# HGRN scores: copies of keys and queries for levels up to 32 tokens, and one run of matmuls for all levels of a pair of heads

## The chip, the cores and the metric

The kernel runs on one core of a Trainium2 chip. The metric is the device time in microseconds (us); before is the median of 3 runs. The engines each work through their own instructions in a fixed order and wait for each other by semaphores: PE is TensorE (matmuls; PEld is its loading of weights), DVE is VectorE, ACT is ScalarE, POOL is GpSimd, and SP issues the transfers (DMA).

## What is computed

A trunk of four residual layers over 256 tokens of width 1024: a token mixer, a layer norm, a SwiGLU block, a layer norm. The mixers are HGRN2, mLSTM, S5 and HGRN2 again, so the code of this change runs in the first and in the last layer. For HGRN2, a gated linear recurrence with 8 heads of 128, the reference forms in each chunk the scores that the kernel's `hgrn_scores` makes:

```python
b = jnp.cumsum(lfb, axis=2)
diff = b[:, :, :, None, :] - b[:, :, None, :, :]
decay = jnp.exp(jnp.where(mask[:, :, None], diff, -jnp.inf))
att = jnp.einsum('bhtd,bhsd,bhtsd->bhts', qb, kb, decay)
o = jnp.einsum('bhts,bhse->bhte', att, vb) + jnp.einsum('bhtd,bhde->bhte', qb * jnp.exp(b), s_prev)
```

The score of a query t and a key s is a dot product in which every one of the 128 channels is damped by the product of its forget gates between s and t. All is float32.

## The kernel before

The 256 tokens are two halves of 128. The heads are taken in four pairs; `q`, `k` and `f` of a pair are tiles of 128 channels x 512 (half, head of the pair, token). The products of gates are built by doubling. At level m (1, 2, 4, ... 64) the tokens fall into blocks of 2m; keys in the first m tokens of a block meet queries in the last m. Ahead of the level, keys hold the gates up to the end of their m tokens and queries those from the start of theirs, so that the level's scores are plain dot products. After it, DVE multiplies half the keys and half the queries by their neighbour's whole product (`mul(x, x, whose(...))`, in place, 128x256 each), and `e`, the products of whole blocks, is halved in length.

In `hgrn_scores` of before, a generator that gives up control after every level:

- The diagonal (key and query the same token) is 16 small matmuls into a bank (L649) and a masked multiply into `near` (L650).
- For m under 32, ACT copies the level's keys into `kk` (L659), TensorE does eight matmuls with 32 key columns and 32 query columns (L663) into a bank of their own, reading the queries with a stride straight from `q`, and DVE puts them under a mask into `near` (L666).
- For m = 32 and 64, eight small matmuls (L672) read `k` and `q` themselves; ACT copies the result into `att` (L679). At m = 32 DVE also copies the diagonal blocks from `near` into `att` (four 32x128 copies, L675).
- At m = 64 DVE multiplies the last half block; then two full 128x128 matmuls (L695) make the scores between the halves, which ACT copies out (`cross`, L697).

In the hardware's count a float32 matmul is two instructions, so eight matmuls show as x16.

`scores` runs the generators of two pairs of heads side by side: a step of one, a step of the other, then a piece of other TensorE work ("fill"): the queries of pairs 2 and 3 and the second half of the values v in the first call (pairs 0 and 1); `heads_out(0)` (att and cross times v, L543 and L545) and eight pieces of the output gate g in the second (pairs 2 and 3). Then come `turn` (gated heads transposed into `oh` and `ol`, L451 and L293), `heads_out(1)` and the output projection (L180 to L182 with `oh`, `ol`).

Weights come in transfers of 1 MB into tiles `w` (three buffers). ACT casts each half to `hi` (L149) and DVE takes the rest as `lo` (L150), eight buffers each; a wide product is three matmuls, L180 to L182. The order on each engine is made when the program is built, by a scheduler that may move instructions within their dependences; on the chip each engine keeps to it.

Of the kernel before, what the change touches and what calls it, by code (L numbers as in the profile page):

```python
# [9 lines left out]
F32 = mybir.dt.float32  # L10
F32R = mybir.dt.float32r
BF16 = mybir.dt.bfloat16
I32 = mybir.dt.int32
AF = mybir.ActivationFunctionType
# [3 lines left out]
P = 128  # L18
D = 1024
S = 256  # L20
KD = D // P
# [5 lines left out]
LN_EPS = 1e-5  # L27
HEAD_EPS = 1e-6
MASKED = (1, 2, 4, 8, 16)
BIG = 1e30  # L30
AHEAD = 1
ROWS = (0, 1, NBLK - 1)
# [2 lines left out]
class Trunk:  # L35
# [448 lines left out]
    def hgrn(self, j, gb, lb=None):  # L484

        nc, tc = self.nc, self.tc
        nw = self.const.tile([P, 1], F32, name=f"hnw{j}")
        with tc.tile_pool(name=self.uid("hg"), bufs=1, reuse_waits="tile") as hp, \
                tc.tile_pool(name=self.uid("hw"), bufs=2, reuse_waits="tile") as wp:
            msk = hp.tile([P, len(MASKED) + 1, 64], F32, name=self.uid("msk"))  # L490
            atts = [hp.tile([P, 512], F32, name=self.uid("att")) for _ in range(3)]
            for t in atts:
                nc.gpsimd.memset(t, 0.0)
            ot = self.transposed(hp)
            v = hp.tile([P, 2, D], F32, name=self.uid("v"))
            g = hp.tile([P, 2, D], F32, name=self.uid("g"))

# [61 lines left out]
            def turn(n, h):  # L559
                o, gate = on[n, h], g[:, h, n * 512 : (n + 1) * 512]  # L560
                nc.vector.tensor_tensor(o, o, gate, ALU.mult)
                self.head_turn(o, n, h, nw, ot, h == 1)

            mem, q, pre, on = {}, {}, {}, {}
# [8 lines left out]

            def scores(prs, fill):

                runs = [self.hgrn_scores(wp, q[pr], *pre[pr], msk, atts[pr % 3]) for pr in prs]
                for todo in fill:
                    for pr, run in zip(prs, runs):
                        mem[pr] = next(run)
                    for f in todo:  # L580
                        f()
# [11 lines left out]
            v1 = pieces(v, AF.Copy, 0, 1)  # L593
            g0, g1 = (pieces(g, AF.Silu, 12, n) for n in range(2))
            scores((0, 1), ([], [lambda: query(2)], [], [lambda: query(3)], v1[0:1], v1[1:2], v1[2:3], v1[3:]))
            late = []
            scores((2, 3), ([lambda: late.append(heads_out(0))], g0[0:1], g0[1:2] + [lambda: late.pop()()], g0[2:3], g0[3:], g1[0:1], g1[1:2], g1[2:3]))
            gb = gb()
            g1[3]()
            for h in range(2):  # L600
                turn(0, h)
            heads_out(1)()
# [19 lines left out]
                act(y, y, AF.Copy, scale=lb[:, 1, hd])  # L622
        return k, f

    def hgrn_scores(self, wp, q, k, f, msk, att):

        nc = self.nc
        mul = lambda o, x, y: nc.vector.tensor_tensor(o, x, y, ALU.mult)
        view = lambda t, o, *dims: bass.AP(t.tensor, t.offset + o, [list(t.ap[0])] + [list(d) for d in dims])
        i32 = lambda x: x.bitcast(I32)
        keys = lambda t, m: view(t, 0, (256 + m, 2), (2 * m, P // m), (1, m))
        queries = lambda t, m: view(t, m, (256 - m, 2), (2 * m, P // m), (1, m))
        whose = lambda e, m, s: view(e, s, (2 * P // m + 1 - 2 * s, 2), (2, P // m), (0, m))  # L640
        four = lambda x: x.rearrange("p (a t) -> p a t", a=4)
        heads = lambda x: x.rearrange("p (a t) -> p a t", a=2)
        rows = lambda c: slice(32 * c, 32 * c + 32)
        near = wp.tile([P, P], F32, tag="near", name=self.uid("near"))
        k4, q4, a4 = four(k), four(q), four(att)
        pd = self.bank("a")[:, 0:P]
        for i in range(4):
            for c in range(4):
                nc.tensor.matmul(pd[rows(c), rows(i)], k4[:, i, rows(c)], q4[:, i, rows(c)], start=True, stop=True)  # L649
        nc.vector.tensor_tensor(four(near), four(pd), msk[:, len(MASKED), None, 0:32].broadcast_to([P, 4, 32]), ALU.mult)  # L650
        mul(q, q, f)
        e, ends = f, wp.tile([P, 256], F32, tag="ends", name=self.uid("ends"))
        spare = 0
        for m in (1, 2, 4, 8, 16, 32, 64):
            n = P // (2 * m)
            pl = self.bank("a")
            if m < 32:
                kk = wp.tile([P, 2 * P], F32, tag="kk", name=self.uid("kk"))
                nc.scalar.copy(view(kk, 0, (m, 2), (2 * m, 2 * n), (1, m)), keys(k, m))  # L659
                pl = pl[:, 0:64]  # L660
                for i in range(2):
                    for c in range(4):
                        nc.tensor.matmul(pl[rows(c)].rearrange("p (h a t) -> p a h t", h=2, a=2)[:, i], kk[:, i * P + 32 * c : i * P + 32 * c + 32],  # L663
                                         view(q, i * P + 32 * c + m, (256 - m, 2), (2 * m, 16 // m), (1, m)), start=True, stop=True)
                three = lambda x: x.rearrange("p (h b m) -> p h b m", h=2, m=m)
                nc.vector.copy_predicated(view(near, m, (64 - m, 2), (2 * m, 32 // m), (1, m)), three(i32(msk[:, MASKED.index(m)])), three(pl))  # L666
            else:
                for i in range(2):
                    for c in range(4):
                        h = c * 32 // m % 2  # L670
                        t = 32 * c // (2 * m) * 2 * m + m * (1 - h)
                        nc.tensor.matmul(pl[rows(c), i * m : (i + 1) * m], k4[:, 2 * h + i, rows(c)], q4[:, 2 * h + i, t : t + m], start=True, stop=True)  # L672
                if m == 32:
                    for c in range(4):
                        nc.vector.tensor_copy(a4[rows(c), :, rows(c)], four(near[rows(c)]))  # L675
                for s in range(0, P, m):
                    h = s // m % 2
                    t = s + m * (1 - 2 * h)
                    nc.scalar.copy(a4[s : s + m, 2 * h : 2 * h + 2, t : t + m], heads(pl[s : s + m, 0 : 2 * m]))  # L679
            if m < 64:  # L680
                for x, y in ((keys(k, m), 1), (queries(q, m), 0)):
                    mul(x, x, whose(e, m, y))
                new = ends[:, 0 : 4 * n]
                if m > 1:
                    new, spare = f[:, spare : spare + 4 * n], spare + 4 * n
                mul(new, e[:, 0::2], e[:, 1::2])
                e = new
            else:
                for x, h in ((k4, 0), (q4, 2)):
                    x = x[:, h : h + 2, 0:m]  # L690
                    mul(x, x, e.rearrange("p (a s) -> p a s", s=2)[:, h : h + 2, 1:].broadcast_to([P, 2, m]))
            yield
        pc = self.bank("a")
        for i in range(2):
            nc.tensor.matmul(pc[:, i * P : (i + 1) * P], k4[:, i], q4[:, 2 + i], start=True, stop=True)  # L695
        cross = wp.tile([P, 2, P], F32, tag="cross", name=self.uid("cross"), bufs=3)
        nc.scalar.copy(cross, pc[:, 0:256].rearrange("p (a t) -> p a t", a=2))  # L697
        yield a4, cross
# [744 lines left out]
def consts():  # L1443
    s, c = np.arange(P)[:, None], np.arange(16)[None, :]
    lvl = []
    for m in MASKED:
        t = (c // m) * 2 * m + c % m
# [7 lines left out]
        "c_lvl": np.stack(lvl, 1).astype(np.float32),  # L1455
        "c_caus": np.where(s > t, np.float32(BIG), np.float32(0.0)),
    }
# [59 lines left out]
```

## Time and profile before

| | us |
|---|---|
| time, median of 3 runs | 1255.83 |
| lowest and highest | 1254.95, 1257.53 |
| span of the profiled execution, first to last instruction | 1251.8 |
| DVE multiplies of keys in the scores (48 of 128x256, the line of `mul`, L635) | 19.0 |
| ACT's key copies (40, L659) | 15.4 |
| DVE's masked copies (40, L666) | 10.2 |

Of the profiled execution the profile has only the span; the runs are timed around it. The scores of the first layer start with the diagonal at 52 us from the span's start (pairs 0 and 1) and at 82 us (pairs 2 and 3); the output projection follows at 118 us. In the last layer the diagonal of pairs 0 and 1 is at 971 us. In a row of the groups, the name before the arrow is written and those behind it are read, then come partitions x elements, the number of instructions, their busy time and mean in ns, and the idle time ahead of them with what ended it. A row of the timeline has the start, the duration (from the first start to the last end where several are merged), the engine, the line and the operation.

### The profile page before, as it was taken

Reading aid. Unit: us, or ns where it says so; the run is one execution under the profiler, and the core shown is the slowest. Engines: PE = TensorE matmul, PEld = TensorE weight load, DVE = VectorE, ACT = ScalarE, POOL = GpSimd, SP = SyncE. Lnnn points to the kernel's source line nnn. Section 1 sums busy time; section 2 is a strip of 40 time slices with the busy share of each in tenths; the row PEclk is TensorE's granted clock in tenths of the full one; section 3 lists DMA queues with packets and bytes.
Section 4 is the critical chain, followed back from the end, with each engine's and each line's share of the span. In section 5 each row is a group of like instructions: output and inputs, shape, how many; then the busy total and the mean of one; then the engine's idle time right before and its main releaser. Section 6 shows DMA issues by size and latency. Waiting matters only on the chain.

```text
span 1251.8 us, 21395 instructions
## 1 busy us (share of the span) xinstructions
PE 1234.0 (99%) x8464; PEld 1031.2 (82%) x8464; DVE 957.8 (77%) x1717; ACT 694.6 (55%) x1126; POOL 34.7 (3%) x60
## 2 busy tenths in 40 slices
PE   9999999999999999999998999999999999999997
PEld 7977788888788888888877788888889777888886
DVE  6887889796787799787599786666486887766664
ACT  6755575565467555555444355555359653555551
POOL 0000100000100100000000000000000000000000
PEclk9999999999999999999999999999999999999999
DMA  8733476666373278667556456555456433755530
GB/s 316 298 136 136 148 269 231 213 223 225 109 288 135 102 281 306 235 243 247 218 202 222 169 193 244 189 183 200 168 179 218 154 132 105 266 189 181 197 140 34
DMA packets 50245, 247.91 MB, mean 198 GB/s; under 512 B 6337, under 2 KB 15953, under 8 KB 23777
## 3 DMA queue, kind: packets, MB, share of 16 engines
q1 hardware_dynamic: 50016, 246.46, 54.7%
q8 instruction: 66, 1.08, 0.3%
q14 instruction: 35, 0.28, 0.1%
q0 software_dynamic: 128, 0.09, 0.0%
HBM read 233.94 MB, written 12.58 MB: 197 GB/s over the span
## 4 chain that ended last, share of the span: by engine, by line
PE 90%; DVE 5%; DMA 2%; ACT 2%; issue 0%; SPq 0%; DVEq 0%; ACTq 0%
PE g L210 18%; PE g L180 10%; PE g L182 10%; PE g L181 10%; PE g L213 9%; PE a L180 9%; PE a L181 8%; PE a L182 8%; DVE lo L150 1%; PE a L369 1%; PE t L271 1%; PE a L663 1%; DMA bc<-in_s_bc 1%; PE a L543 1%; DVE s5rot L1217 1%; DMA first<-in_first 1%
## 5 line engine op out<-in xcount | busy, mean ns | idle before, releaser
L150 DVE TENSOR_TENSOR lo<-w,hi 128x1024 fp32r<-128x1024 f32 x388 | 471.2, 1222 | 117.3 <-ACT hi L149 109.9
L149 ACT CAST hi<-w 128x1024 fp32r<-128x1024 f32 x388 | 405.5, 1051 | 187.5 <-PE a L181 100.6
L210 PE MATMUL g<-xx,hi 128*128 128x512 f32 x1024 | 356.7, 394 | 0.4 <-DVE sum L351 0.3
L213 PE MATMUL g<-xx,lo 128*128 128x256 f32 x1024 | 267.2, 281 | 0.0
L210 PEld LDWEIGHTS g<-xx,hi 128*128 128x128 f32 x1024 | 186.3, 188 | 36.1 <-DVE sum L351 1.1
L213 PEld LDWEIGHTS g<-xx,lo 128*128 128x128 f32 x1024 | 192.4, 188 | 11.0
L180 PE MATMUL g<-hi,xx 128*128 128x512 f32 (+1 forms) x416 | 167.5, 404 | 2.5 <-ACT xx L290 2.1
L182 PE MATMUL g<-lo,xx 128*128 128x512 f32 (+1 forms) x416 | 165.2, 399 | 0.1
L181 PE MATMUL g<-hi,xx 128*128 128x512 f32 (+1 forms) x416 | 164.6, 397 | 0.0
L180 PE MATMUL a<-hi,hh 128*128 128x512 f32 x328 | 129.5, 395 | 0.0
L350 ACT COPY sum<-g 128x256 f32<-128x256 f32 x128 | 47.7, 373 | 147.1 <-PE g L210 147.0
L182 PE MATMUL a<-lo,hh 128*128 128x512 f32 x328 | 129.1, 394 | 0.0
L181 PE MATMUL a<-hi,hl 128*128 128x512 f32 x328 | 128.9, 393 | 0.0
L351 DVE TENSOR_TENSOR sum<-g,sum 128x256 f32<-128x256 f32 x128 | 54.2, 423 | 63.5 <-ACT sum L350 62.9
L180 PEld LDWEIGHTS g<-hi,xx 128*128 128x128 f32 x416 | 78.3, 188 | 21.0 <-ACT xx L290 3.5
L182 PEld LDWEIGHTS g<-lo,xx 128*128 128x128 f32 x416 | 78.2, 188 | 18.2 <-DVE lo L150 1.4
L181 PEld LDWEIGHTS g<-hi,xx 128*128 128x128 f32 x416 | 78.4, 188 | 15.8
L182 PEld LDWEIGHTS a<-lo,hh 128*128 128x128 f32 x328 | 61.5, 188 | 14.5
L181 PEld LDWEIGHTS a<-hi,hl 128*128 128x128 f32 x328 | 61.5, 188 | 14.4 <-DVE hl L340 0.3
L180 PEld LDWEIGHTS a<-hi,hh 128*128 128x128 f32 x328 | 61.5, 188 | 12.6 <-ACT hh L339 0.2
L180 PE MATMUL g<-xx,hi 128*128 128x256 f32 x192 | 54.5, 284 | 0.0
L182 PE MATMUL g<-xx,hi 128*128 128x256 f32 x192 | 54.3, 283 | 0.0
(307 smaller groups left out, 1730.4 us busy)
## 6 DMA issues: line engine op xcount, KB each, us to landing
w<-in_w_gu SPq DMA_DIRECT2D x88, 1024.0 KB
w<-in_w_dn SPq DMA_DIRECT2D x44, 1024.0 KB
w<-in_w_hg SPq DMA_DIRECT2D x30, 1024.0 KB
w<-in_w_ml SPq DMA_DIRECT2D x12, 1024.0 KB
gb<-in_ln SPq DMA_DIRECT2D x8, 1024.0 KB
w<-in_w_ho SPq DMA_DIRECT2D x8, 1024.0 KB
w<-in_w_so SPq DMA_DIRECT2D x8, 1024.0 KB
w<-in_w_mo SPq DMA_DIRECT2D x4, 1024.0 KB
```

The costliest lines, as they stand in the source:

```text
L149: self.nc.scalar.copy(hi, x)
L150: i = self.nc.vector.tensor_tensor(lo, x, hi.bitcast(F32), ALU.subtract).ins
L180: mm(ps, lh, rh, start=start, stop=False)
L181: mm(ps, ll, rh, start=False, stop=False)
L182: mm(ps, lh, rl, start=False, stop=stop)
L210: whole = lambda: mm(ps, hi[:, c], self.xx[:, k].rearrange("p i t -> p (i t)"), start=k == 0, stop=k == KD - 1)
L213: mm(ps[:, S:], lo[:, c], self.xh[:, k], start=False, stop=False)
L271: nc.tensor.transpose(pt[:, (k % 4) * P : (k % 4 + 1) * P], z[:, k * P : (k + 1) * P], self.ident)
L350: nc.scalar.copy(t, ps[:, S:])
L351: nc.vector.tensor_tensor(t, ps[:, 0:S], t, ALU.add)
L369: nc.tensor.matmul(down[h][n], hidden(h, j, b)[x], dn[j][b][y][:, f], start=False, stop=(x, y, b) == steps[-1])
L543: nc.tensor.matmul(o, att[:, 2 * h + hd % 2, :], v[:, h, c], start=True, stop=h == 0)
```

## The change

Levels up to 32 (`NEAR`) no longer go to TensorE one by one. ACT copies the level's keys (as before) and now also its queries, into a tile of their own for each level: `big` (four levels, 2048 wide; named lev) and `kk` (two levels, 1024 wide). DVE multiplies `k` and `q` in place once they are copied. When the last multiply stands in the schedule, all matmuls of the pair follow: eight for m = 64, then eight for each of the six levels, 56 in all, into one bank at different columns. `self.order(...)` only tells the scheduler to place them behind that multiply. Then the masked copies for m under 32, the copies into `att` (those from `near` now on ACT instead of DVE) and, in place of DVE's two last multiplies, four on ACT (activation with a scale per channel). The generator still stops eight times. `big` shares its buffers with `oh` and `ol`, so these are made after the scores.

```diff
@@ def hgrn @@
-            ot = self.transposed(hp)
...
+            ot = tuple(hp.tile([P, KD, S], F32R, tag="o", name=self.uid(n), bufs=2) for n in ("oh", "ol"))
             for h in range(2):
                 turn(0, h)
@@ def hgrn_scores @@
+        big = hp.tile([P, 2048], F32, tag="o", name=self.uid("lev"), bufs=2)
+        kk = wp.tile([P, 1024], F32, tag="kk", name=self.uid("kk"))
+        saved = [t[:, i * 256 : (i + 1) * 256] for t, n in ((big, 8), (kk, 4)) for i in range(n)]
...
-        for m in (1, 2, 4, 8, 16, 32, 64):
+        for g, m in enumerate(NEAR):
             n = P // (2 * m)
...
+            kc, qc = saved[2 * g : 2 * g + 2]
+            nc.scalar.copy(view(kc, 0, (m, 2), (2 * m, 2 * n), (1, m)), keys(k, m))
+            nc.scalar.copy(view(qc, 0, (P, 2), (m, 2 * n), (1, m)), queries(q, m))
+            for x, y in ((keys(k, m), 1), (queries(q, m), 0)):
+                last = mul(x, x, whose(e, m, y)).ins
...
             yield
+        pl = self.bank("a")
+
+        def tiny(o, x, y):
+            self.order(nc.tensor.matmul(o, x, y, start=True, stop=True).ins, last)
+
+        for i in range(2):
+            for c in range(4):
+                h = c // 2
+                t = 64 * (1 - h)
+                tiny(pl[rows(c), 384 + i * 64 : 448 + i * 64], k4[:, 2 * h + i, rows(c)], q4[:, 2 * h + i, t : t + 64])
+        for g, m in enumerate(NEAR):
...
+                    tiny(o, x, y)
+        for g, m in enumerate(MASKED):
+            three = lambda x: x.rearrange("p (h b m) -> p h b m", h=2, m=m)
+            nc.vector.copy_predicated(view(near, m, (64 - m, 2), (2 * m, 32 // m), (1, m)), three(i32(msk[:, g])), three(pl[:, 64 * g : 64 * g + 64]))
+        for c in range(4):
+            nc.scalar.copy(a4[rows(c), :, rows(c)], four(near[rows(c)]))
+        for m, o in ((32, 320), (64, 384)):
...
+                nc.scalar.copy(a4[s : s + m, 2 * h : 2 * h + 2, t : t + m], heads(pl[s : s + m, o : o + 2 * m]))
+        for x, h in ((k4, 0), (q4, 2)):
+            for i in range(h, h + 2):
+                nc.scalar.activation(x[:, i, 0:64], x[:, i, 0:64], AF.Copy, scale=e[:, 2 * i + 1 : 2 * i + 2])
+        yield
```

The order that the scheduler makes of it, at three places of the first layer. TensorE in the first call of `scores`, before (`a` is a bank, the numbers tell tiles apart; q_559 is pair 0, q_620 pair 1; L180 to L182 are wide matmuls of the values):

```order
L663 MATMUL a_906<-q_559,kk_907 32x2x16 x8
L663 MATMUL a_921<-q_620,kk_922 32x2x16 x8
L180 MATMUL g_937<-hi_851,xx 128x512
L181 MATMUL g_937<-hi_851,xx 128x512
L182 MATMUL g_937<-lo_852,xx 128x512
L672 MATMUL a_960<-q_559,k_280 32x32 x8
L180 MATMUL g_936<-hi_940,xx 128x512
L672 MATMUL a_980<-q_620,k_349 32x32 x8
L181 MATMUL g_936<-hi_940,xx 128x512
```

And the same call now (L674 is the run; q_557 and lev_621 are pair 0, q_618 and lev_649 pair 1; the wide matmuls are L181 to L183 by the new file's lines):

```order
L183 MATMUL g_839<-lo_774,xx 128x512
L674 MATMUL a_884<-q_557,k_278 32x64 x8
L674 MATMUL a_884<-lev_621 32x2x16 x32
L674 MATMUL a_884<-kk_622 32x2x16 x8
L674 MATMUL a_884<-kk_622 32x32 x8
L674 MATMUL a_960<-q_618,k_347 32x64 x8
L674 MATMUL a_960<-lev_649 32x2x16 x32
L674 MATMUL a_960<-kk_650 32x2x16 x8
L674 MATMUL a_960<-kk_650 32x32 x8
L181 MATMUL g_838<-hi_842,xx 128x512
```

All level matmuls of the two pairs follow each other, with no wide matmul between; the queries of pairs 2 and 3 and half of the values have moved ahead of them.

DVE at the end of the second call, now (k_485 and q_826 are pair 3, near_1082 pair 2, on the heads' output, g the gate; before, each masked copy stood ahead of the next level's multiplies):

```order
L636 TENSOR_TENSOR k_485<-k_485,f_486 128x2x4x32
L636 TENSOR_TENSOR q_826<-q_826,f_486 128x2x4x32
L151 TENSOR_TENSOR lo_1489<-w_1486,hi_1488 128x1024
L151 TENSOR_TENSOR lo_1493<-w_1486,hi_1492 128x1024
L561 TENSOR_TENSOR on_1218<-on_1218,g_155 128x512
L561 TENSOR_TENSOR on_1220<-on_1220,g_155 128x512
L151 TENSOR_TENSOR lo_1581<-w_1578,hi_1580 128x1024
L695 COPY_PREDICATED near_1082<-msk_147,a_1312 128x2x32
L151 TENSOR_TENSOR lo_1585<-w_1578,hi_1584 128x1024
L695 COPY_PREDICATED near_1082<-msk_147,a_1312 128x2x16x2
L151 TENSOR_TENSOR lo_1603<-w_1600,hi_1602 128x1024
L695 COPY_PREDICATED near_1082<-msk_147,a_1312 128x2x8x4
```

The masked copies have moved behind the last multiplies and behind weights of the output projection. ACT at the same place, before (L679 copies into att, g is the gate, oh the turned heads):

```order
L679 COPY att_150<-a_1376 32x2x32 x4
L679 COPY att_148<-a_1396 32x2x32 x4
L149 CAST hi_1602<-w_1600 128x1024
L679 COPY att_150<-a_1440 64x2x64 x2
L679 COPY att_148<-a_1453 64x2x64 x2
L149 CAST hi_1606<-w_1600 128x1024
L697 COPY cross_1481<-a_1478 128x256
L697 COPY cross_1486<-a_1483 128x256
L149 CAST hi_1640<-w_1638 128x1024
L93 ACTIVATE g_157<-g_1416 128x512
L149 CAST hi_1644<-w_1638 128x1024
L93 ACTIVATE g_157<-g_1417 128x512
```

And now (L705 is the scaling that DVE did, L697 and L702 the copies into att, L711 cross):

```order
L705 ACTIVATE k_485<-k_485,f_486 128x64 x2
L705 ACTIVATE q_826<-q_826,f_486 128x64 x2
L697 COPY att_150<-near_1082 32x4x32 x4
L702 COPY att_150<-a_1312 32x2x32 x4
L702 COPY att_150<-a_1312 64x2x64 x2
L697 COPY att_148<-near_1110 32x4x32 x4
L702 COPY att_148<-a_1388 32x2x32 x4
L702 COPY att_148<-a_1388 64x2x64 x2
L711 COPY cross_1479<-a_1476 128x256
L711 COPY cross_1484<-a_1481 128x256
L150 CAST hi_1606<-w_1600 128x1024
L150 CAST hi_1640<-w_1638 128x1024
```

All copies into att stand in one row behind the scalings, and two casts of the output projection's weights have moved behind them.

More of the change, by code (lines that the diff above doesn't have):

```diff
@@ L29 @@
 MASKED = (1, 2, 4, 8, 16)
+NEAR = MASKED + (32,)
 BIG = 1e30
@@ L574, in scores @@
             def scores(prs, fill):
-                runs = [self.hgrn_scores(wp, q[pr], *pre[pr], msk, atts[pr % 3]) for pr in prs]
+                runs = [self.hgrn_scores(hp, wp, q[pr], *pre[pr], msk, atts[pr % 3]) for pr in prs]
                 for todo in fill:
@@ L623, in hgrn_gates, with hgrn_scores @@
         return k, f
-    def hgrn_scores(self, wp, q, k, f, msk, att):
+    def hgrn_scores(self, hp, wp, q, k, f, msk, att):
         nc = self.nc
@@ L652, in hgrn_scores @@
         e, ends = f, wp.tile([P, 256], F32, tag="ends", name=self.uid("ends"))
-        spare = 0
-        for m in (1, 2, 4, 8, 16, 32, 64):
+        spare, last = 0, None
+        for g, m in enumerate(NEAR):
             n = P // (2 * m)
[L656 to L691, printed above, removed]
-            yield
@@ new lines, in hgrn_scores @@
+            kc, qc = saved[2 * g : 2 * g + 2]
[3 more added lines that the diff above has]
+                last = mul(x, x, whose(e, m, y)).ins
+            new = ends[:, 0 : 4 * n]
+            if m > 1:
+                new, spare = f[:, spare : spare + 4 * n], spare + 4 * n
+            mul(new, e[:, 0::2], e[:, 1::2])
@@ new lines, in hgrn_scores @@
+            e = new
+            yield
+        pl = self.bank("a")
[7 more added lines that the diff above has]
+        for g, m in enumerate(NEAR):
+            kc, qc = saved[2 * g : 2 * g + 2]
+            for i in range(2):
+                for c in range(4):
+                    x = kc[:, i * P + 32 * c : i * P + 32 * c + 32]
+                    o = pl[rows(c), 64 * g : 64 * g + 64]
+                    if m < 32:
+                        o = o.rearrange("p (h a t) -> p a h t", h=2, a=2)[:, i]
+                        y = view(qc, (4 * i + c) * 16, (P, 2), (1, 16))
+                    else:
+                        o, y = o[:, rows(i)], qc[:, c % 2 * P + (2 * i + c // 2) * 32 :][:, 0:32]
+                    tiny(o, x, y)
@@ new lines, in hgrn_scores @@
+        for g, m in enumerate(MASKED):
+            three = lambda x: x.rearrange("p (h b m) -> p h b m", h=2, m=m)
+            nc.vector.copy_predicated(view(near, m, (64 - m, 2), (2 * m, 32 // m), (1, m)), three(i32(msk[:, g])), three(pl[:, 64 * g : 64 * g + 64]))
+        for c in range(4):
+            nc.scalar.copy(a4[rows(c), :, rows(c)], four(near[rows(c)]))
+        for m, o in ((32, 320), (64, 384)):
+            for s in range(0, P, m):
+                h = s // m % 2
+                t = s + m * (1 - 2 * h)
+                nc.scalar.copy(a4[s : s + m, 2 * h : 2 * h + 2, t : t + m], heads(pl[s : s + m, o : o + 2 * m]))
```

## Prediction

> **What bounds the kernel now.** The page comes first: how long, which engine is busy, and what the chain of waits ends on.
>
> ```profile
> span 1251.8 us, 21395 instructions
> PE 1234.0 (99%) x8464; PEld 1031.2 (82%) x8464; DVE 957.8 (77%) x1717; ACT 694.6 (55%) x1126; POOL 34.7 (3%) x60
> PE 90%; DVE 5%; DMA 2%; ACT 2%; issue 0%; SPq 0%; DVEq 0%; ACTq 0%
> ```
>
> TensorE sets the end: 99% busy, 90% of the chain. So an edit pays only if it shortens TensorE's own sequence, and costs only if TensorE comes to wait. The groups show little to gain: the level matmuls of the scores are busy for 11.1 us in 640 instructions (two per matmul).
>
> ```profile
> L663 PE MATMUL a<-q,kk 128*32 128x32 f32 x640 | 11.1, 200 | 0.0
> ```
>
> But a busy mean of pipelined matmuls hides what lies between two starts. The timeline of TensorE shows it, around a group of 16 such instructions, one of 32, and one of 32 with 64 columns (start, duration):
>
> ```profile
> 94.75 0.40 PE L181 MATMUL g<-hi,xx 128*128 128x512 f32 x1
> 95.07 0.46 PE L663 MATMUL a<-q,kk 128*32 128x32 f32 x32
> 95.46 0.50 PE L182 MATMUL g<-lo,xx 128*128 128x512 f32 x1
> 95.80 0.39 PE L180 MATMUL g<-hi,xx 128*128 128x512 f32 x1
> 96.03 0.39 PE L181 MATMUL g<-hi,xx 128*128 128x512 f32 x1
> ...
> 98.57 0.40 PE L181 MATMUL g<-hi,xx 128*128 128x512 f32 x1
> 98.90 0.33 PE L663 MATMUL a<-q,kk 128*32 128x32 f32 x16
> 99.16 0.50 PE L182 MATMUL g<-lo,xx 128*128 128x512 f32 x1
> 99.50 0.39 PE L180 MATMUL g<-hi,xx 128*128 128x512 f32 x1
> ...
> 104.05 0.40 PE L182 MATMUL g<-lo,xx 128*128 128x512 f32 x1
> 104.38 0.65 PE L672 MATMUL a<-q,k 128*32 128x64 f32 x32
> 104.96 0.50 PE L180 MATMUL g<-hi,xx 128*128 128x512 f32 x1
> 105.30 0.39 PE L181 MATMUL g<-hi,xx 128*128 128x512 f32 x1
> ```
>
> Two wide matmuls start 0.23 us apart (95.80 to 96.03). With a group of 16 between, three starts span 98.57 to 99.50: 0.93 less two wide intervals is 0.47 us. With 32, 94.75 to 95.80 gives 0.59. So 16 more cost 0.12 (7.5 ns each), and **entering and leaving the narrow shape costs 0.33 to 0.35 us** whatever the group's size; I take 0.33. By the same fixed part, the 64-column group (1.25 - 0.46 = 0.79) costs 14 ns an instruction.
>
> **The change part by part.** *Fewer switches.* In the order of before, the two calls of the scores of a layer enter the narrow shape 12 and 11 times; in the new order 3 and 3 times (the diagonal blocks of two pairs of heads in one or two groups, one run for both pairs; in the second call one or a few matmuls of the run stand alone). The instructions are as many as before: 32 + 96 + 16 a pair. The full-size cross matmuls are wide and pay no switch in either. So 17 x 0.33 = 5.6 us a layer, **11.2 us in both**, if nothing waits.
>
> *What must be ready at the run.* Instead of one level's copy, the run needs all six rounds of ACT copies and DVE multiplies of both pairs. Marks of before, then DVE and ACT at work there (start to start is what a row occupies):
>
> ```profile
> 52.18 0.46 PE L649 MATMUL a<-q,k 128*32 128x32 f32 x32
> ...
> 58.55 0.28 PE L181 MATMUL a<-xx,lo 128*128 128x256 f32 x1
> ...
> 64.00 0.28 PE L182 MATMUL a<-xx,hi 128*128 128x256 f32 x1
> ...
> 82.31 0.46 PE L649 MATMUL a<-q,k 128*32 128x32 f32 x32
> ...
> 117.81 0.48 PE L180 MATMUL g<-hi,oh 128*128 128x512 f32 x1
> ...
> 123.50 0.63 PE L451 MATMUL t<-ident,on 128*128 128x128 f32 x4
> ```
>
> ```profile
> 52.71 0.29 DVE L650 TENSOR_TENSOR near<-a,msk 128x128 f32<-128x128 f32 x1 [0.99 <-PE a L649]
> 52.92 0.68 DVE L635 TENSOR_TENSOR q<-q,f 128x512 f32<-128x512 f32 x1
> 53.52 0.42 DVE L635 TENSOR_TENSOR k<-k,f 128x256 f32<-128x256 f32 x1
> 53.85 1.22 DVE L150 TENSOR_TENSOR lo<-w,hi 128x1024 fp32r<-128x1024 f32 x1
> ```
>
> ```profile
> 64.82 0.70 ACT L659 COPY kk<-k 128x256 f32<-128x256 f32 x2
> 65.42 1.05 ACT L149 CAST hi<-w 128x1024 fp32r<-128x1024 f32 x1
> 66.37 0.40 ACT L659 COPY kk<-k 128x256 f32<-128x256 f32 x1
> ```
>
> DVE, both pairs: twice 0.21 + 0.60, 24 multiplies of 0.33, one lo of 1.2, and some 1.5 for the ten smaller products of the ends: 12.2 us, with 0.5 of waits for ACT 12.7, so to 65.4. ACT's 22 copies at 0.30 to 0.33 and two or three casts at 0.95 take 9 to 10 us beside it. TensorE now does queries 2 and 3 first: 96 matmuls at 0.12 ((64.00 - 58.55) / 46), 24 wide ones at 0.23 and the diagonal blocks, 18.3 us, so it is at the run at 70.4, with 5 us in hand. In the last layer one piece of v stands before the diagonal blocks, which takes 3.0 us of this cover: 2 us in hand. First runs: nothing.
>
> *Behind the first run.* ACT holds a cast until TensorE has freed its buffer (70.4). Then come 8 scalings 128x64, two key copies, 8 copies 32x128, 8 of 32x64, 4 of 64x128, a cast and two cross copies, and heads_out of the next call wants att and cross. The 32x64 and 64x128 copies are in the trace; the 32x128 copy stood on DVE (0.22), and the scaling was DVE's 128x128 multiply, half as often.
>
> ```profile
> L675 DVE COPY att<-near 32x128 f32<-32x128 f32 x32 | 6.9, 216 | 0.3
> ...
> 74.52 1.72 ACT L679 COPY att<-a 32x64 f32<-32x64 f32 x8
> ...
> 77.34 1.09 ACT L679 COPY att<-a 64x128 f32<-64x128 f32 x4
> L93 ACT ACTIVATE k<-k,lb 128x256 f32<-128x256 f32 x8 | 3.9, 494 | 0.0
> ```
>
> A scaling lies between 0.22 (the 32x64 copy) and 0.49 (four times the elements with a scale); I take 0.25, near the copy, 0.27 for the 32x128 copy. Sum 0.95 + 2.0 + 0.7 + 2.2 + 1.7 + 1.1 + 0.95 + 0.7 = 10.3, to 80.7. TensorE arrives at 80.0 and needs the first cross 0.9 later: no wait, but no slack; at 0.49 a scaling it waits 1.7.
>
> *Second run.* DVE's new chain stands behind a lo that waits for the cast after those copies, so it begins near 81 and, with two reductions and two scalings of heads_out among its rows, reaches the last multiply of pair 2 after 12.5 to 13.5 us, 94. TensorE arrives after heads_out (2.7) and 54 wide matmuls (12.6) at 95.4: no wait in layer 0. In the last layer the cast comes later against TensorE's place (v's evictions ahead of it) and a lo stands among the last multiplies: there 2 us of wait.
>
> *The tail.* After the second run DVE does five lo and two gate products (8 us) before the ten masked copies end; ACT then has both pairs' copies (5.0), two crosses, three casts, two gates and the first oh: 10.2 us from 103.4, so oh comes at 113.6. TensorE, 5.2 us ahead of before by then, wants it at 112.8 and ol 0.6 after: 1.2 to 1.5 us of wait, against none before (117.81 follows heads_out at once). From there oh, the squares, their reductions and GpSimd's power set the next turn:
>
> ```profile
> 121.46 1.29 DVE L555 TENSOR_TENSOR on<-a,rs 128x512 f32<-128x512 f32 x2 [2.05 <-POOL rs L223]
> ```
>
> that turn (123.50 before) I put at 120.0, so 3.5 us are kept in layer 0; in the last layer 5.6 - 2 - 1.3 = 2.3.
>
> *A long narrow run* can outrun TensorE's instruction supply, as in the S5 layer:
>
> ```profile
> 655.06 1.09 PE L1201 MATMUL g<-s5u,bm 128*32 128x64 f32 x63
> 656.79 1.23 PE L1201 MATMUL g<-s5u,bm 128*32 128x64 f32 x65 [0.64 <-issue]
> ```
>
> Nothing at best (a run of 128 elsewhere has no gap), 0.64 in each of four runs at worst, 2.6 us; where TensorE waits for the tail anyway it is hidden. I take 0.2 net. DVE loses 32 copies and 16 multiplies, covered by TensorE either way. The output tiles oh and ol move into the level buffers and are written after both runs: nothing.
>
> **Sum.** 11.2 less 2.1 (layer 0), 3.3 (last layer) and 0.2 leaves 5.6 us: span 1251.8 to 1246.2. The runs shown (1254.95 to 1257.53, median 1255.83) lie 4.0 over the span, so **1250.2 us**.
>
> **Rivals.** *The tail takes it all.* If what now stands behind a run on ACT costs more (0.49 for each of 8 scalings, 0.15 more for each of 16 small copies: 4.3 us), oh comes as late as 117.81 and both layers end where they did: 1255.8. For it speaks that the small copies of two pairs lay among the levels' casts and gates and now all wait for the run; against it, that oh has 4 us to lose. The Trainium skill, "TensorEngine Tiling (Array Packing)", section PSUM Bottleneck, says that packing speeds up TensorE but not the emptying of PSUM, which may become the bottleneck, and advises both ScalarE and VectorE for it, where this change puts more on ScalarE; by that rule the time is this rival's. No row of before shows the emptying as TensorE's bound there, which is why it gets the smaller chance.
>
> *Slower: the chain paces.* Each multiply must wait for ACT's copy of the same round, and each copy for the round before. I have two pairs overlap fully (1.6 us a round). If a weight cast in ACT's queue and the hand-overs make a round 2.4, six rounds grow by 4.8: with 5, 1.4, 2 and -2 us in hand, TensorE waits 0, 3.4, 2.8 and 6.8, 13 us against 11.2 gained, with the tail's 2.6: about 1260. It turns slower from a round of 2.2 on. Against it: a copy and a multiply of one tensor take 0.40 + 0.42, so even one pair alone turns in under 1.6.
>
> *It keeps nearly all.* If ACT's scalings and copies are as short as 0.2 and the casts fall in gaps, the waits vanish: 1244.6 to 1247.
>
> *Same work, same switches.* If the 0.33 belonged to waits for the copies and not to the shape, merging would save little: 1254 to 1256. Against it: 16 and 32 instructions give the same fixed part.
>
> **Chances.** Forecast (1247 to 1253.3) 0.50; nearly all kept 0.17; eaten by the tail or no switch cost 0.23; slower 0.10. A measurement tells 0.2%, 2.5 us, from no change: faster 0.67, same 0.23, slower 0.10. The range leaves out the very best and the slow case: 1245 to 1257.
>
> **What would show it.** Right: 12 entries into the narrow shape instead of 46; the second call beginning near 80.0 instead of 82.31 and out_proj near 114 with a wait of about 1 us for oh; 2 us before the last layer's second run. Wrong: waits of over 2 us at a run for q or k; a narrow instruction at over 8 ns in a run; gaps of issue within it; heads_out waiting for att or cross; or oh at 117 or later.

## The result, and the profile after

| | us |
|---|---|
| before, median of 4 runs beside it | 1255.66 (1254.95 to 1257.53) |
| after, median of 4 runs | 1264.87 (1262.25 to 1265.97) |
| ratio | 1.0073, 95% interval 1.0060 to 1.0086 |
| predicted | 1250.2, range 1245 to 1257 |

The change makes the kernel slower by 9.2 us, where 5.6 us of gain were forecast. The profiled execution has a span of 1262.1 us against 1251.8. Its page, the lines that answer to the first three of before:

```profile
span 1262.1 us, 21401 instructions
PE 1228.8 (97%) x8464; PEld 1033.9 (82%) x8464; DVE 947.3 (75%) x1669; ACT 728.3 (58%) x1246; POOL 39.1 (3%) x60
PE 81%; DVE 8%; ACT 4%; DMA 3%; issue 2%; POOL 1%; SPq 0%; DVEq 0%; ACTq 0%; POOLq 0%
```

TensorE has as many instructions as before and is busy for 5 us less, but its share of the chain fell from 90% to 81%: it now waits. "Issue", time in which it waited for nothing that the profile names, rose from 0% to 2%. The waits of TensorE's queue, longest in total first (what waited, for what, total us, times, longest):

```profile
PE a L674 <- issue: 8.7, 2, 4.6
PE g L181 <- ACT g L94: 4.4, 2, 3.2
...
PE a L653 <- ACT att L702: 1.2, 1, 1.2
...
PE a L709 <- issue: 0.6, 1, 0.6
PE t L452 <- DVE on L561: 0.3, 1, 0.3
```

L674 is the line of the run. Two of its four runs, both in the first layer, stop in the middle. The timeline of TensorE around the first of them:

```profile
76.71 0.39 PE L674 MATMUL a<-kk 128*32 128x32 f32 x21 [4.16 <-issue]
77.02 0.79 PE L181 MATMUL g<-hi,xx 128*128 128x512 f32 x1
77.61 0.63 PE L182 MATMUL g<-hi,xx 128*128 128x512 f32 x1
78.04 0.63 PE L183 MATMUL g<-lo,xx 128*128 128x512 f32 x1
78.47 0.63 PE L181 MATMUL g<-hi,xx 128*128 128x512 f32 x1
...
80.75 0.39 PE L181 MATMUL g<-hi,xx 128*128 128x512 f32 x1
```

A run of both pairs leaves 448 records, 224 of matmuls and 224 of weight loads; 21 of the matmul records were still to come when TensorE stood for 4.16 us. The layer's second run stops further from its end:

```profile
111.33 0.38 PE L674 MATMUL a<-lev 128*32 128x32 f32 x11 [4.56 <-issue]
```

Behind the first gap the wide matmuls start 0.43 us apart (77.61 to 78.04), not 0.23. The same stretch by windows (the length, the busy us and instructions of PE, PEld, DVE, ACT and POOL, then the granted TensorE clock, the share of DMA time and GB/s):

```profile
70.00:72.00 2.00, 2.00 (x165) 1.79 (x164) 1.94 (x3) 1.86 (x5) 0.00 (x0) 1.00 0.93 336
72.00:74.00 2.00, 0.55 (x57) 0.43 (x47) 1.64 (x6) 1.90 (x8) 0.00 (x0) 1.00 1.00 406
74.00:76.00 2.00, 0.00 (x0) 0.00 (x0) 0.00 (x0) 1.83 (x8) 0.00 (x0) 1.00 1.01 389
76.00:78.00 2.00, 1.29 (x23) 1.10 (x24) 0.79 (x3) 0.55 (x3) 0.00 (x0) 0.75 0.42 176
78.00:80.00 2.00, 2.00 (x6) 1.57 (x5) 0.50 (x3) 1.30 (x5) 0.00 (x0) 0.50 0.05 12
80.00:82.00 2.00, 2.00 (x11) 1.69 (x11) 0.00 (x0) 1.81 (x7) 0.00 (x0) 0.90 0.00 0
```

Two things are to be seen. The DMA engines are full (1.00) for as long as TensorE stands, with weights. And after the gap the clock is granted at 0.50 until about 80, which costs another 1.6 us (eight starts in 3.50 us, 77.02 to 80.52, where 1.9 would do). So the second call of the scores begins late:

```profile
52.08 0.46 PE L653 MATMUL a<-q,k 128*32 128x32 f32 x32
...
85.23 0.76 PE L653 MATMUL a<-q,k 128*32 128x32 f32 x64
...
126.06 0.48 PE L181 MATMUL g<-hi,oh 128*128 128x512 f32 x1
...
979.26 0.95 PE L653 MATMUL a<-q,k 128*32 128x32 f32 x64
...
1043.64 0.47 PE L181 MATMUL g<-hi,oh 128*128 128x512 f32 x1
```

From the first diagonal to the output projection the first layer takes 73.98 us (65.63 before), the last 64.38 (62.57 before, 971.17 to 1033.74): 8.35 and 1.81, together 10.2, where the span grew by 10.3. The switches were saved: 6 and 5 entries into the narrow shape instead of 23 and 23, 11.6 us at 0.33. Lost were 8.7 in the two gaps, about 4 in half clock (behind both gaps and behind the wait of 3.2), 5.6 in waits for ScalarE (4.4 for a gate activation, 1.2 for att) and 0.9 more (0.6 and 0.3). That makes 7.6 of 10.2. The 2.6 us that are left may lie in the price of a switch: at 0.28 us, as experiment 8 shows it, 9.8 are saved and not 11.6, and 0.8 are left.

### The profile page after: what moved, and what is told of

The parts are those of the page before. It is cut to its first block, busy times and chain, and to the rows that moved or that the text cites. A ratio compares the mean times of both kernels' runs of the same rounds, so it can differ in the third digit from the quotient of the medians.

```text
span 1262.1 us, 21401 instructions
## 1 busy us (share of the span) xinstructions
PE 1228.8 (97%) x8464; PEld 1033.9 (82%) x8464; DVE 947.3 (75%) x1669; ACT 728.3 (58%) x1246; POOL 39.1 (3%) x60
## 4 chain that ended last, share of the span: by engine, by line
PE 81%; DVE 8%; ACT 4%; DMA 3%; issue 2%; POOL 1%; SPq 0%; DVEq 0%; ACTq 0%; POOLq 0%
PE g L211 18%; PE g L214 9%; PE g L181 8%; PE g L183 8%; PE g L182 8%; PE a L182 8%; PE a L181 8%; PE a L183 8%; DVE lo L151 2%; ACT hi L150 1%; PE a L370 1%; PE t L272 1%; DMA bc<-in_s_bc 1%; PE a L674 1%; DVE s5rot L1231 1%
## 5 line engine op out<-in xcount | busy, mean ns | idle before, releaser
L181 PE MATMUL g<-hi,xx 128*128 128x512 f32 (+1 forms) x416 | 168.9, 407 | 6.9 <-ACT g L94 4.4
L182 PE MATMUL g<-hi,xx 128*128 128x512 f32 (+1 forms) x416 | 165.1, 398 | 0.0
L183 PE MATMUL g<-lo,xx 128*128 128x512 f32 (+1 forms) x416 | 164.9, 398 | 0.1
L181 PE MATMUL a<-hi,hh 128*128 128x512 f32 x328 | 129.5, 395 | 0.0
L183 PE MATMUL a<-lo,hh 128*128 128x512 f32 x328 | 129.2, 394 | 0.0
L182 PE MATMUL a<-hi,hl 128*128 128x512 f32 x328 | 128.8, 393 | 0.0
L181 PEld LDWEIGHTS g<-hi,xx 128*128 128x128 f32 x416 | 79.3, 191 | 26.7 <-ACT g L94 5.3
L183 PEld LDWEIGHTS g<-lo,xx 128*128 128x128 f32 x416 | 79.2, 191 | 18.9 <-DVE lo L151 1.4
L182 PEld LDWEIGHTS g<-hi,xx 128*128 128x128 f32 x416 | 79.4, 191 | 16.1
L183 PEld LDWEIGHTS a<-lo,hh 128*128 128x128 f32 x328 | 61.5, 188 | 14.5
L182 PEld LDWEIGHTS a<-hi,hl 128*128 128x128 f32 x328 | 61.5, 188 | 14.3 <-DVE hl L341 0.2
L181 PEld LDWEIGHTS a<-hi,hh 128*128 128x128 f32 x328 | 61.5, 188 | 12.5 <-ACT hh L340 0.2
L181 PE MATMUL g<-xx,hi 128*128 128x256 f32 x192 | 54.5, 284 | 0.1
L183 PE MATMUL g<-xx,hi 128*128 128x256 f32 x192 | 54.3, 283 | 0.0
```

The lines of the kernel that those rows point to most:

```text
L181: mm(ps, lh, rh, start=start, stop=False)
L182: mm(ps, ll, rh, start=False, stop=False)
L183: mm(ps, lh, rl, start=False, stop=stop)
```

## The experiments

**The theories.** F (fetch): TensorE's instructions themselves come by DMA, in blocks, and a long run of short instructions uses up what is loaded while the next block waits behind weights. Its page row is

```profile
q8 instruction: 66, 1.08, 0.3%
```

66 packets of 16 KB for TensorE's 2 x 8464 = 16,928 records: 256 instructions a packet. The run of two pairs is 448 instructions in 2.4 us; wide ones would last 256 x 0.117 = 30 us. The windows from the span's start to either gap count what TensorE had issued (matmuls and weight loads):

```profile
0.00:72.60 72.60, 71.16 (x732) 63.26 (x732) 56.47 (x92) 57.44 (x94) 1.79 (x9) 1.00 0.77 284
0.00:106.80 106.80, 100.00 (x1112) 86.48 (x1113) 79.20 (x151) 82.00 (x159) 6.10 (x11) 0.98 0.60 222
```

1464 and 2225: 761 apart, three blocks of 256 less a few records that a trace can miss. The gaps stand at the same place of a block. Up to the first gap the instruction queue had moved four packets, up to the second seven: three more here too. Rivals: L (length: any long run of narrow matmuls stalls), W (a wait that the profile doesn't name, at those matmuls), and C (the extra copies on ScalarE are the real loss, and the gaps stand where TensorE would wait anyway).

The table has all runs; the second and third columns are the time from the first diagonal to the output projection in the first and last layer, read from the timelines as above.

| | first layer | last layer | median | ratio to before, 95% |
|---|---|---|---|---|
| before | 65.63 | 62.57 | 1254.6 to 1255.7 | |
| after | 73.98 | 64.38 | 1264.87 | 1.0073 (1.0060 to 1.0086) |
| 1 shifted | 69.67 | 67.83 | 1262.97 | 1.0061 (1.0046 to 1.0076) |
| 2 halves | 67.20 | 64.45 | 1260.60 | 1.0038 (1.0025 to 1.0051) |
| 3 loads held | 70.19 | 64.41 | 1262.14 | 1.0058 (1.0042 to 1.0075) |
| 4 no run, all copies | 66.42 | 70.02 | 1264.90 | 1.0079 (1.0064 to 1.0094) |
| 5 levels by twos | 62.92 | 60.13 | 1250.27 | 0.9963 (0.9949 to 0.9978) |
| 6 halves, less on ScalarE | 65.99 | 60.33 | 1253.65 | 0.9984 (0.9975 to 0.9994) |
| 7 run, less on ScalarE | 73.81 | 61.07 | 1262.52 | 1.0062 (1.0046 to 1.0078) |
| 8 levels by twos and three | 61.78 | 58.81 | 1247.77 | 0.9941 (0.9924 to 0.9958) |

The intervals of 1, 3, 4 and 7 overlap that of after: there the verdict is read from the trace, not from the time.

**1. The run shifted against the blocks.**

```diff
     for _ in range(9):
         self.nc.tensor.matmul(ps, z[:, 0:P], z, start=True, stop=True)
+    for _ in range(78):
+        self.nc.tensor.matmul(ps[0:32, 0:32], z[:, 0:32], z[:, 0:32], start=True, stop=True)
```

> 156 more TensorE instructions (78 narrow bf16 matmuls) stand in the warm-up at the start; nothing else differs from the changed kernel. Theory F (fetch): TensorE's instructions come in blocks of 256 (packets of 0.02 MB on the instruction queue), a run of 448 uses them up in 2.4 us, and the next block waits its turn behind the weight loads on the DMA engines. In the changed kernel both gaps of layer 0 stand at a block's end (406 and 354 instructions into the run). Moved by 156, the first run begins 250 before a block's end and runs short only after 506, more than it has: its gap of 4.2 us and the half clock behind it (1.6 us) go. The second run's shortage moves from 354 to 454, behind its last instruction, and stands at the wide matmuls there, some 3 us. In all about 1258. Theory L (length): any run of over some 400 narrow instructions stalls; both gaps stay at 4.2 and 4.6 us, 1264 to 1266. Theory W (a wait that the profile doesn't name): both gaps stay at the same matmuls, 1264 to 1266.

The instructions of the first layer's runs are the same, 60 us and more after the added ones. The first run's last row and the next gap:

```profile
73.17 0.45 PE L676 MATMUL a<-kk 128*32 128x32 f32 x30
73.55 0.50 PE L183 MATMUL g<-hi,xx 128*128 128x512 f32 x1
...
108.47 0.59 PE L185 MATMUL g<-lo,xx 128*128 128x512 f32 x1 [2.89 <-issue]
```

The first run goes through, the second call begins at 80.22 instead of 85.23, and the second shortage has moved behind the run to a wide matmul, 2.89 us where 3 were expected. It stands at 2481 instructions, one block of 256 behind the 2225 of before the shift. L and W, by which nothing moves, fall: it is the place in the block that counts. The time was missed (1263.0 for 1258): the working had left out the last layer, whose two runs went through before and now ran short themselves, by 4.86 and 2.03 us. A shift only deals the gaps out anew.

**2. The run in two halves.** One piece of projections between the two pairs' matmuls:

```diff
-for todo in fill:
+for n, todo in enumerate(fill):
     for pr, run in zip(prs, runs):
         mem[pr] = next(run)
-    for f in todo:
+        if n < 6 or pr != prs[0]:
+            continue
+        for f in todo:
+            f()
+    for f in todo if n < 6 else ():
         f()
```

> The changed kernel with one piece of projections (12 wide matmuls, 2.8 us) between the run's two pairs of heads. F: 224 instructions, 24 wide ones in 2.8 us, 224 again: the shortage comes 4.8 us after the run's start and the block lands about 6.3 us after it, so a gap of at most 1.5 us in place of 4.2 and no half clock; one more switch (0.33) per run: 1255 to 1259. L: 224 is under the limit, no gap at all: 1254 to 1256. W: the gap stays about 4 us at the same matmul of the second pair: 1263 to 1266.

The gaps shrink to 1.35 and 1.21 us in the first layer and the clock stays whole there, but they don't vanish, though no half is longer than 224 instructions: against L again. The time is 1.6 us over the range given: the shortage came back behind the diagonals, at the first matmuls of heads_out, which the working had not counted: 1.51 us in the first layer and 2.25 in the last, both with the DMA engines idle (share 0.00).

**3. The weight loads held back.**

```diff
...
+self.hold = atts[1]
...
+if name == "w_ho" and self.hold and tuple(at) in ((0, 0), (0, 1)):
+    self.nc.vector.tensor_copy(st[0:1, 0:1], self.hold[0:1, 0:1])
 self.nc.sync.dma_start(st[:, 0 : src.shape[-1]], src)
```

> The changed kernel, but the first two weight loads of the output projection of layer 0 (1 MB each), which start as the first run starts, are held until the att copies behind that run; TensorE's, ScalarE's and SyncE's instructions and their order are the same, VectorE has two 1x1 copies more. F: the block's fetch finds the DMA engines free, so the first run's gap shrinks from 4.2 us to under 1 and the half clock behind it goes: layer 0's second call 5 us earlier, 1258 to 1260; the second run's gap stays unless its place against the loads moves. L and W: the first gap stays at 4.2 us: 1264 to 1266.

The same run, with the DMA engines nearly idle (share 0.03) while TensorE stands; first the windows, then TensorE's timeline:

```profile
70.00:72.00 2.00, 2.00 (x157) 1.64 (x157) 1.94 (x3) 1.69 (x5) 0.00 (x0) 1.00 0.73 307
72.00:74.00 2.00, 0.65 (x70) 0.54 (x56) 1.81 (x6) 1.93 (x8) 0.00 (x0) 1.00 0.03 8
```

```profile
72.39 0.27 PE L678 MATMUL a<-kk 128*32 128x32 f32 x9
74.26 0.39 PE L678 MATMUL a<-kk 128*32 128x32 f32 x21 [1.61 <-issue]
74.58 0.50 PE L184 MATMUL g<-hi,xx 128*128 128x512 f32 x1
```

TensorE stops at the same matmul, 21 before the end, but for 1.61 us instead of 4.16, and the clock stays at 1.00. The instruction packet shows up in the DMA queue at 72.1 us instead of 74.5 (where the queue's count of packets rises), and TensorE goes on 2.2 us after it either way. So the weights are 2.5 us of the gap, and 1.6 are left without them, more than the 1 expected. The second call began 4.0 us earlier (81.22); the second run's gap, whose loads were not held, stayed at 4.53. In the changed kernel that gap too ends behind its packet, which shows up at 109.0 us, 2.3 us before TensorE goes on.

**4. All copies, no run.** Each level's eight matmuls right behind their copies:

```diff
             nc.scalar.copy(view(qc, 0, (P, 2), (m, 2 * n), (1, m)), queries(q, m))
+            for i in range(2):
+                for c in range(4):
+                    ...
+                    tiny(o, x, y)
...
-        for g, m in enumerate(NEAR):
-            ...
-                    tiny(o, x, y)
```

> All copies of the changed kernel, one bank per pair, and its burst of copies at the end, but each level's 8 matmuls go to TensorE right behind their copies, as before the change; only the run is gone. F and L: no gaps and no half clock (11.9 us less), but most of the switches are back (11.2 us gain falls to some 2 to 5): 1259 to 1262. Rival C (the copies and their burst on ScalarE are the loss, the gaps only stand where TensorE would have waited anyway): 1265 or more, with waits for ScalarE in place of the gaps.

Here F's number is wrong and C's right to 0.1 us: 1264.9. There is no gap of issue in the scores, and 17 entries a layer instead of 23, yet both layers are longer than before, the last by 7.5 us. Half clock, which was to be gone, came back there behind two waits for ScalarE (3.35 and 2.13 us, then 0.50). The waits of TensorE now name ScalarE:

```profile
PE a L707 <- ACT q L703: 4.0, 2, 2.1
...
PE g L181 <- ACT v L522: 3.4, 1, 3.4
```

L703 is the scalings at the end, L522 an activation of v that stands behind the copies. So the copies and their burst are a loss of their own, which the gaps partly hide in the changed kernel.

**5. Levels by twos.** From the kernel of before: in each two of levels only the first has its queries copied, the second reads them from `q` itself; the copies into att and the last multiplies stay as they were.

```diff
-for m in (1, 2, 4, 8, 16, 32, 64):
+for m, m2 in ((1, 2), (4, 8), (16, 32)):
...
+    save(kk, m, True)
+    last = step(m)
+    if m2 < 32:
+        save(kk[2:], m2, False)
+    due.append(last)
+    yield
+    level(pl[:, 0:64], m, kk[:2])
+    level(pl[:, 64:128], m2, kk[2:])
...
+    last = step(m2)
```

> The kernel of before with levels taken two at a time (1 with 2, 4 with 8, 16 with 32, then 64 alone), both pairs of heads side by side; only the first level of each two has its queries copied (six more copies on ScalarE per call of the scores), the copies out of PSUM and the last multiplies stay where they were before the change. No group has more than 128 TensorE instructions, and pieces of projections stand between. TensorE enters the narrow shape 10 times a layer instead of 23. Theory F (fetch): no gap in any group, so the switches' 0.33 us comes through: 13 x 0.33 x 2 = 8.6 us less, less 0 to 4 us of waits for ScalarE's copies: 1247 to 1251. Rival C (the extra copies and waits on ScalarE eat what the switches give): 1253 to 1258. Rival S (the switch costs nothing by itself): 1255 or more with no new waits in the trace.

1250.27, in F's range: 11 entries a layer, no gap, and at the groups two waits of 0.3 and 0.4 us for VectorE. It is 0.37% faster than before, so the switches do cost time (against S), though this got 5.15 us in the two layers for 24 entries fewer, 0.21 each, and not 0.33.

**6 and 7. The burst on VectorE.** In the halved run and in the whole one:

```diff
-            nc.scalar.copy(a4[rows(c), :, rows(c)], four(near[rows(c)]))
+            nc.vector.tensor_copy(a4[rows(c), :, rows(c)], four(near[rows(c)]))
...
-            for i in range(h, h + 2):
-                nc.scalar.activation(x[:, i, 0:64], x[:, i, 0:64], AF.Copy, scale=e[:, 2 * i + 1 : 2 * i + 2])
+            x = x[:, h : h + 2, 0:64]
+            mul(x, x, e.rearrange("p (a s) -> p a s", s=2)[:, h : h + 2, 1:].broadcast_to([P, 2, 64]))
```

> The halved run of the experiment before, with the 32x128 copies from near to att and the last scalings of keys and queries back on VectorE (one multiply each instead of two activations), as they were before the change. If ScalarE's queue behind the run is what holds att and the gate activations, the waits of TensorE for them (1.5 and 0.7 us there) go and the time falls by 1 to 3 us, to 1257 to 1260. If the queue of level copies ahead of the gate holds them, or if VectorE, now with more to do, comes late with the next call's multiplies, it stays at 1260 to 1262.

> The changed kernel with its whole run, and only the 32x128 copies and the last scalings back on VectorE: the ScalarE part alone, without the split. If the moved ScalarE work and the fetch gaps are separate losses, the gaps stay (two of 4 to 5 us with the half clock behind them) and the time falls about as far as in the halved run, where the same edit took 7 us: 1257 to 1260. If the gaps cover that work in the changed kernel, 1262 to 1265.

In the halved run the edit took 7 us by the medians and 5.3 by the two layers of the profiles, more than the 1 to 3 expected. The waits for att and oh went; those for the gate, which were to go too, grew from 1.5 to 2.4 us. Not all of the gain is ScalarE's time: the shortage at heads_out shrank from 1.51 us to nothing in the first layer and from 2.25 to 0.97 in the last, and the half clock behind it went; why it shrank is not shown. In the whole run the gaps stay as they were:

```profile
76.72 0.45 PE L674 MATMUL a<-kk 128*32 128x32 f32 x21 [4.16 <-issue]
...
111.17 0.38 PE L674 MATMUL a<-lev 128*32 128x32 f32 x11 [4.42 <-issue]
...
1021.86 0.51 PE L181 MATMUL g<-hi,xx 128*128 128x512 f32 x1 [2.05 <-ACT g L94]
```

The first layer, which has the gaps, gains 0.2 us, and the last, which has none, 3.3. That is the cover: ScalarE works its burst off while TensorE stands in the gap (busy for 1.90 and 1.83 of 2.00 us in the two windows of the gap above). The gate waits fall only from 4.4 to 3.3 us, since they come from the level copies ahead of the gate, which this edit leaves where they are.

**8. Twos and a three.** As 5, with 16, 32 and 64 in one group (keys and queries of 32 copied too):

```diff
+    else:
+        yield
+        save(kk[2:], m2, True)
+        last = step(m2)
...
+    if m2 == 32:
+        level(pl[:, 128:256], 64, None)
```

> The kernel of levels taken two at a time, but 16, 32 and 64 in one group (keys and queries of 32 copied too, two more copies): groups of up to 192 instructions, some 9 entries into the narrow shape a layer instead of 11. Theory F: 192 is under a block of 256, so no gap inside a group; 1 to 1.5 us less than the twos: 1248 to 1251. If a group of 192 already runs short, a gap of 1 us or more shows in it and the time is 1251 to 1255.

The group of both pairs in the first layer, 192 instructions:

```profile
72.76 0.46 PE L669 MATMUL a<-kk 128*32 128x32 f32 x32
73.03 0.43 PE L669 MATMUL a<-q,k 128*32 128x64 f32 x15
...
73.29 0.47 PE L669 MATMUL a<-kk 128*32 128x32 f32 x30
...
73.59 0.44 PE L669 MATMUL a<-q,k 128*32 128x64 f32 x15
73.96 0.50 PE L180 MATMUL g<-hi,xx 128*128 128x512 f32 x1
```

No gap, and no wait of TensorE in the scores stands in its list of waits (0.2 us and over). 1247.77 us, 0.59% (0.42 to 0.76) faster than before: the version that beats both kernels. The layers are 3.85 and 3.76 us shorter than before with 27 entries fewer, 0.28 us for each.

## Why the prediction was wrong

*Fewer switches*: right. 11 entries instead of 46 (12 were forecast). In the two kernels without a gap in the scores an entry saved 0.21 us (experiment 5, with two short waits in it) and 0.28 (experiment 8), not quite the 0.33 of the timeline.

*What must be ready at the run*: right. The first run began at 70.21 (70.4 forecast) with no wait for q or k, and the last layer's first run had none either.

*Behind the first run*: the place was right, the wait was not. Without the gap the second call began at 80.22 (experiment 1, where the added matmuls put the first diagonal 0.9 us later; 80.0 forecast). But "no wait, but no slack" came out as a wait for the first cross:

```profile
81.82 1.35 PE L545 MATMUL a<-v,att 128*128 128x128 f32 x10 [0.84 <-ACT cross L713]
```

In the changed kernel the gap hides this wait in the first layer. In the last, whose first run has no gap, att was 1.2 us late.

*Second run*: 2 us of wait were forecast in the last layer and none in the first, and the place was wrong. The run itself never waited for a multiply. What waited was a bank of the output gate, whose activation stood in ScalarE's queue behind the level copies, 1.2 us in the first layer and 3.2 in the last:

```profile
1022.78 0.80 PE L181 MATMUL g<-hi,xx 128*128 128x512 f32 x1 [3.18 <-ACT g L94]
```

ScalarE and VectorE ahead of it:

```profile
1017.84 1.29 DVE L555 TENSOR_TENSOR on<-a,rs 128x512 f32<-128x512 f32 x2 [1.81 <-POOL rs L224]
...
1019.49 0.41 ACT L661 COPY kk<-k 128x256 f32<-128x256 f32 x1 [2.21 <-DVE k L636]
...
1022.14 0.59 ACT L94 ACTIVATE g<-g 128x512 f32<-128x512 f32 x1
```

The level copies themselves waited for VectorE's multiplies, and these stood behind two products of heads_out that waited for GpSimd. The working followed DVE's chain to the run and not to what ScalarE's copies are ahead of.

*The tail*: no wait for oh showed, since TensorE itself came late (126.06 against about 114); the 3.5 us that were to be kept in the first layer became 8.35 lost. What experiments 6 and 7 gave back to VectorE took 7 us in the halved run and was mostly hidden in the changed kernel itself. The Trainium skill, "TensorEngine Tiling (Array Packing)", section PSUM Bottleneck, which the prediction names beside the tail's rival, advises both ScalarE and VectorE for emptying PSUM. No run here tests that: the copies from `near` and the scalings that moved read no PSUM bank.

*A long narrow run can outrun TensorE's instruction supply*: **the step that failed**. The mechanism was named, and mis-sized: 0.2 us net, 0.64 a run at worst, from the one gap of the S5 layer. It measured 4.16 and 4.56 us in two runs, none in the other two, and 1.6 and 1.2 us of half clock behind the two (the latter 112.12 to 114.71, six starts in 2.59 us), 11.5 us in all. The gap that the price came from was not the only one on record; the list of TensorE's waits before has four of issue, all in the S5 layer and none over 0.8 us:

```profile
PE t L1247 <- issue: 2.2, 3, 0.8
PE g L1201 <- issue: 0.6, 1, 0.6
```

Above all, a price taken from there left out what sets it: where in its block the run begins (experiment 1), and what the DMA engines carry just then (experiment 3, 2.5 of 4.2 us). Without these 11.5 us the time would have been about 1253.4, inside the range and 3.2 over the forecast; but then the gaps would have hidden nothing of ScalarE's work either (experiments 4 and 7). Gaps of issue within a run were among the signs that the prediction had named for being wrong. Its rival on the slower side, at 0.10, was another mechanism (multiplies that pace the chain): in the changed kernel no run waited for a multiply.

*The last layer* shows that a second, smaller term was short. The first layer came out 11.9 us worse than forecast (8.35 lost for 3.5 gained), which the gaps and their half clock fill. The last came out 4.1 us worse (1.81 lost for 2.3 gained) with no gap in its runs: there 3.3 us of waits were forecast, and 3.2 and 1.2 came for ScalarE, with some 1.3 of half clock behind the longer one and 0.6 of issue. The rest may lie in the price of a switch.

## What to carry to other kernels

Merge groups of small matmuls to save TensorE's switches, but bound the group: up to 192 instructions with several us of wide work behind them ran clean in all four places here, and a run of 448 stopped in two of four. Whether 192 would run clean wherever it stands in its block was not tried. Look at the instruction queue's packets and at which weight loads start beside such a run, and expect the gaps to move when anything ahead of them changes the instruction count. And when copies are added so that work can be merged, follow the queue of the engine that gets them: what stands behind them there, such as an activation that frees a bank, becomes the next wait.

## What the runs showed of the hardware

- TensorE's instruction stream can be the bound. It ran dry with the DMA engines full of weights (4.16 and 4.56 us at shares of 0.99 and 0.92) and, for 1.5 to 2.3 us, with them nearly empty (experiments 2 and 3). The Trainium skill, "Runtime: NRT & Kernel Launch", section Instruction fetch mechanics, says that an engine loads its instructions in blocks of 256 over a DMA queue while it runs, and that this is mostly hidden. The blocks agree with 256 instructions a packet here; hidden it was not.
- After TensorE had stood for 2.9 us or more (2.89, 3.18, 4.16 us), the clock was granted at 0.50 for 2 us or more. After gaps of 1.2 to 1.87 us it stayed at 1.00 in every run. In between it went either way: 2.03 and 2.43 us kept it (experiment 1), 2.05 (experiment 7), 2.13 (experiment 4) and 2.25 (experiment 2) lost it; what decides there is not shown. The Trainium skill, "TensorE: Matmul & The Clock Gate", Part 1, states half the clock after an idle window of about 3.4 us that runs freely. The gaps over 4 us agree with it; those from 2.05 to 3.18 us are shorter than such a window and lost the clock all the same.
- Still open: why TensorE stands for 1.5 to 2.3 us even with the DMA engines nearly empty, and why it goes on only 2.2 us after its packet.
